# A two-layer attention trunk on one core: turned keys and queries kept as scaled fp16 pairs, key pairs copied by DMA

## The chip, the cores and the metric

The kernel runs on one core of a Trainium2 chip. The metric is the device time of one execution in microseconds; a quoted time is the median of several runs. Beside the timed runs stands one profiled execution, from which all rows in this document come.

## The reference, cut to what matters

Two layers over 512 latent tokens (8 x 64) and 256 context tokens, width 1024, all in fp32. Each layer normalises its input, modulates it, and multiplies it by one wide matrix `w_in`; the product holds keys, values and queries of two attentions (heads of 64), the silu paths and the merge gates.

```
hx = rmsnorm(x, g) * (1 + scale) + shift;  px = hx @ w_in          # hc, pc likewise for the context
qa, ka = rmsnorm(a_q, q_norm_a), rmsnorm(a_k, k_norm_a)            # 8 heads
s = [ qa . ka(window 8 x 16) / 8 + bias  |  qa . cka / 8 ]         # A: neighbourhood and context keys
a = softmax(s) @ values
qb, kb = rope(rmsnorm(b_q, q_norm_b)), rope(rmsnorm(b_k, k_norm_b))  # 8 query heads, 2 key heads
b = softmax(qb . [ckb, kb] / 8) @ values                           # B: all latent and context keys
out = (sigmoid(g_a) * ((a * silu(a_z)) @ w_o_a) + sigmoid(g_b) * ((b * silu(b_z)) @ w_o_b)) @ w_out
x = x + gate * out
```

In layer 0 the context tokens go through the same (they read context keys only); layer 1 updates the latent tokens alone.

## The kernel before, in words

All 768 tokens of a layer stay in SBUF, as six tiles of 128 tokens, already normalised and transposed, each number as a pair of fp32r tiles, high and low (`hx`). Weights come in tiles of 128 x 512 (`load_w`, L397, and `load_w2`, L412): SyncE's DMA queue (SP) loads `raw`, ScalarE casts it to `whi`, and VectorE or GpSimd subtracts for `wlo`. A projection takes three matmuls for each of eight weight tiles (`mm3`, L433): high by high, high by low, low by high.

The order within a layer, and what carries it in the code:

- **Projections of attention A** (from L705): the keys for the six token tiles, the values (`C_AV`, from L756), the queries (`C_AQ`, from L767). A tile's sums of squares go through ScalarE, VectorE and GpSimd (`head_rstd`, L510), then VectorE scales the heads, and the tile is put on a list of late work. `turn` (L524) is that late work: four TensorE transposes into a PSUM tile of the pool "t" (two buffers), and one ScalarE pass that writes fp32 channels by tokens into `ka` or `qa`, with the norm's weight as scale. `perm` shifts the latent queries by 64 tokens, so that tiles 0 and 3 are written in two pieces.
- **Attention A** (`pipeline`, L1013, with `na_first` L1034): head by head, the scores of head h and then the values of head h - 1, with chunks of other projections as fill between them. For each head `stage_k` (L865) makes fp32r pairs of the keys from `ka`, in one of two pairs of tiles, and `stage_q` (L874) a tile whose one half holds the high part of the head's queries and whose other half holds the low part; `kh` is written twice, once for each half of the 128 rows, so that one matmul by `kh` gives the high and the low query part, and one by `kl` adds the low key part (`scores`, L883, and L974). `load_bias` (L948) loads the head's relative position bias; VectorE adds it and takes the maximum (L977), ScalarE takes the exponential, and the probabilities are split into fp16 halves (`turned`, L831) and turned by transposing DMAs on SP's queue. In layer 0 each head has context scores as well (`ctx_scores`, L892).
- **Projections of attention B** (from L1064): keys and values (`evac_bkv`, L1085), then the queries (`evac_bq`, L1120), with the rotary turn in `rope_heads` (L578). `stage_k` runs once for each of the two key heads, after query tiles 1 and 2, and fills `gk`.
- **Attention B** (L1148 to L1201): the same pipeline, with `stage_q` for each head, scores over all 768 keys, and the maximum against the constant `lift` (L1157).
- **Merge and output** (from L1204).

Beside this, steps of the adaLN product run in the background: `ada_steps` (L278) loads a tile of `w_ada` (`rawb`, two buffers) on SP's queue and reduces it on VectorE, behind the VectorE instruction issued last (`behind`, L473). In layer 0 the steps for the output gate come in two halves, one beside the projections of B (L1099), one in attention B (L1200). Their loads have no such order, neither before nor after the change.

In `start` (L1287) each engine keeps the order of the program. Everywhere else a planner, which goes through the program with a simulated timeline, orders the instructions of every engine and of the DMA queues, and gives out the buffers: of 9 tiles of 128 x 3072 fp32 (`big`, L91) each tensor such as `ka`, `va`, `qa`, `za`, `vb` or `gk` takes one.

Of the kernel before, what the change touches and what calls it, by code (L numbers as in the profile page):

```python
# [34 lines left out]
P_UP = 2.0 ** 14  # L35
SPLIT_POOL = (1, 3)
# [20 lines left out]
def F(ap):  # L57
    return ap.bitcast(F32)
# [14 lines left out]
def hybrid_kernel(es: ExitStack, tc, x, ctx, cvec, w_ada, w_ada0, small, gvec, w_in, w_o_a, w_o_b, w_out,  # L73
# [56 lines left out]
    cd = drp.tile([16, 128], F32, name="cd")  # L130
    gs = [drp.tile([128, 4, NTOK], F32, name=f"gs{c}") for c in range(4)]
# [55 lines left out]
    G.memset(ehalf, -0.5)  # L187
# [39 lines left out]


# [295 lines left out]
    def turn(y, npair, dst, t, perm, g):  # L524

        n = 128 * npair
        pt = psw(n, "t")
        for j in range(npair):
            T.transpose(pt[:, 128 * j:128 * j + 128], y[:, 128 * j:128 * j + 128], ident)
        if perm and t in (0, 3):  # L530

            src = pt.rearrange("p (j s n) -> p j s n", j=npair, s=2)
            d = dst[:, :, 0:512].rearrange("p j (s n) -> p j s n", n=64)
            if t == 0:
                d = d[:, :, 0:3:2, :]
            else:
                src, d = src[:, :, ::-1, :], d[:, :, 1:8:6, :]
        else:
            c0 = 128 * t + (64 if perm and t < 4 else 0)
            src = pt.rearrange("p (j n) -> p j n", j=npair)  # L540
            d = dst[:, :, c0:c0 + 128]
        if g is None:
            S.copy(d, src)
        else:
            S.activation(d, src, AF.Copy, scale=g)
# [49 lines left out]
    def layer(l, hx, nxt, start):  # L595
# [110 lines left out]
        kav = big("ka").rearrange("p (j n) -> p j n", j=4)  # L706
        if first:
# [7 lines left out]
            def evac_ak(ts):  # L715
# [9 lines left out]
                for i, t in enumerate(ts):  # L725
                    mul_heads(ys[t], ys[t], ss[:, 8 * i:8 * i + 8], 8)
                    to_channels(ys[t], 4, kav, t, False, gk)
# [3 lines left out]
        else:  # L731
# [3 lines left out]
            for t in range(6):  # L735
                tok_proj(w, 512, a_hx, t, evac_na(kav, False, gk, 4))
# [19 lines left out]
        w = load_w(W, C_AV, 512, KT, mix_lo)  # L756
        for t in range(6):
            tok_proj(w, 512, a_hx, t, evac_va)
            if first:
# [6 lines left out]
        qav = big("qa").rearrange("p (j n) -> p j n", j=4)  # L766
        w = load_w(W, C_AQ, 512, KT, mix_lo, own=hp["p"])  # L767
        za = big("za")
# [6 lines left out]
        for t in range(qt):  # L775
            tok_proj(w, 512, a_hx, t, evac_na(qav, True, gq, YB if first else 4))
# [10 lines left out]
        if True:  # L787
# [68 lines left out]
            def k_tile(e, zero):  # L856
                kh = att["p"].tile([128, 768], F32R, tag=f"kh{e}", name=nm("kh"), bufs=1)
                kl = att["p"].tile([128, 768], F32R, tag=f"kl{e}", name=nm("kl"), bufs=1)
                if zero:
                    V.tensor_scalar(rows(kl, 1 - e).rearrange("p (a b) -> p a b", b=128),  # L860
                                    rows(ident, 1 - e).unsqueeze(1).to_broadcast([64, 6, 128]),
                                    0.0, None, ALU.mult)
                return kh, kl

            def stage_k(src, e, kh, kl, dup):  # L865

                k = rows(src, e)
                V.tensor_copy(rows(kh, e), k)
                S.copy(rows(kh, 1 - e), k)
                (G if dup else V).tensor_tensor(rows(kl, e), k, F(rows(kh, e)), ALU.subtract)  # L870
                if dup:
                    S.copy(rows(kl, 1 - e), F(rows(kl, e)))

            def stage_q(src, e):  # L874

                n = 768 if first else 512
                qs = att["p"].tile([128, n], F32R, tag=f"qs{e}", name=nm("qs"), bufs=1)
                q = rows(src, e)[:, :n]
                S.copy(rows(qs, e), q)
                V.tensor_tensor(rows(qs, 1 - e), q, F(rows(qs, e)), ALU.subtract)  # L880
                return qs
# [10 lines left out]
            def ctx_scores(q, kh, kl, ct, late=True):  # L892
# [7 lines left out]
                if late:  # L900
# [625 lines left out]
```

## Time and profile before

| | us |
|---|---|
| median of 3 runs | 1111.63 (1110.95 to 1113.45) |
| the profiled execution | 1110.55 |
| its span, first to last instruction | 1108.8 |
| TensorE busy in it | 1074.5 (97%) |
| VectorE busy | 767.4 (69%) |
| ScalarE busy | 617.2 (56%) |
| GpSimd busy | 470.1 (42%) |

Times in rows are us from the start of the span, and ns where a row gives the mean or the minimum, median and maximum of one instruction. PE is TensorE's matmul, PEld its weight load, DVE VectorE, ACT ScalarE, POOL GpSimd, SPq the queue of SyncE. L974 is line 974 of the kernel before. A row of a line or tile reads: line, engine, operation, out<-in by the program's names, count, duration. In brackets stands how long the engine had been idle and what ended that. Matmuls overlap, so the distance between two of them, not the duration of one, is what the stream costs.

### The profile page before, as it was taken

To read this page: it belongs to the slowest core of one execution; us is meant where nothing else is said; L and a number is where in the kernel's file an instruction comes from. 1 tells how busy PE (TensorE), PEld (TensorE's weight loads), DVE (VectorE), ACT (ScalarE), POOL (GpSimd) and SP (SyncE) were. 2 spreads that over 40 slices of the span, in tenths; PEclk is the share of its full clock that TensorE was granted. 3 is DMA by queue.
4 is the path that set the end of the run, shared out by engine and by line. 5 is a ranking of instruction groups with operands and counts; after the bars stand their busy time and mean duration, and the time that the engine had idled before them with its cause. 6 is when DMAs were issued, how large, how long until landed. Compare 5 with 4: busy or idle time off the path is not lost. (4 is left out here: it accounts for less than half of the span.)

```text
span 1108.8 us, 16943 instructions
## 1 busy us (share of the span) xinstructions
PE 1074.5 (97%) x5672; PEld 876.9 (79%) x5672; DVE 767.4 (69%) x1600; ACT 617.2 (56%) x1236; POOL 470.1 (42%) x397
## 2 busy tenths in 40 slices
PE   8999999899999999979999999999999999999998
PEld 6688888788888877757788878888877888777677
DVE  5567799974378478676577785466997665777473
ACT  6464279776333566655330275444899446786430
POOL 1044235554256244454521455232355472564531
PEclk9999999999999999989999999999999999999999
DMA  9454325554543498769533542453565536879642
GB/s 374 153 169 143 91 70 116 125 137 121 174 141 117 132 205 185 172 185 271 171 105 125 166 136 82 138 165 99 132 148 130 156 106 171 200 232 236 188 152 77
DMA packets 236001, 171.79 MB, mean 155 GB/s; under 512 B 160141, under 2 KB 201865, under 8 KB 234249
## 3 DMA queue, kind: packets, MB, share of 16 engines
q1 hardware_dynamic: 228576, 156.31, 51.7%
q0 software_dynamic: 2368, 7.87, 2.2%
q10 hardware_dynamic: 4968, 6.53, 1.8%
q8 instruction: 45, 0.74, 0.3%
q14 instruction: 44, 0.35, 0.1%
HBM read 115.58 MB, written 17.32 MB: 120 GB/s over the span
## 5 line engine op out<-in xcount | busy, mean ns | idle before, releaser
L838 POOL TENSOR_TENSOR h<-p,h 128x256 f16<-128x256 f32 (+2 forms) x104 | 113.1, 1096 | 167.7 <-ACT h L837 119.9
L422 POOL TENSOR_TENSOR wlo<-raw,whi 128x512 fp32r<-128x512 f32 x70 | 98.8, 1416 | 124.5 <-ACT whi L420 80.9
L435 PE MATMUL psf<-hx,whi 128*128 128x512 f32 (+1 forms) x360 | 137.5, 382 | 2.5 <-ACT zt L625 1.3
L437 PE MATMUL psf<-hx,wlo 128*128 128x512 f32 (+1 forms) x360 | 135.5, 376 | 0.0
L436 PE MATMUL psf<-hx,whi 128*128 128x512 f32 (+1 forms) x360 | 135.4, 376 | 0.0
L435 PE MATMUL psx<-whi,hx 128*128 128x512 f32 (+1 forms) x328 | 121.0, 372 | 0.0
L420 ACT CAST whi<-raw 128x512 fp32r<-128x512 f32 x136 | 82.9, 620 | 67.5 <-DMA raw<-in_w_in_dram 48.3
L437 PE MATMUL psx<-whi,hx 128*128 128x512 f32 (+1 forms) x328 | 120.0, 367 | 0.0
L436 PE MATMUL psx<-wlo,hx 128*128 128x512 f32 (+1 forms) x328 | 119.6, 366 | 0.0
L408 POOL TENSOR_TENSOR wlo<-raw,whi 128x512 fp32r<-128x512 f32 x40 | 59.5, 1489 | 119.2 <-ACT whi L405 76.0
L405 ACT CAST whi<-raw 128x512 fp32r<-128x512 f32 x88 | 54.2, 623 | 96.8 <-PE psx L437 34.2
L508 POOL TENSOR_TENSOR ss<-ss,ehalf 128x8 f32<-128x8 f32 (+2 forms) x40 | 63.6, 1593 | 77.8 <-DVE ss L505 72.5
L422 DVE TENSOR_TENSOR wlo<-raw,whi 128x512 fp32r<-128x512 f32 x66 | 70.8, 1073 | 35.2 <-ACT whi L420 34.1
L837 ACT CAST h<-p 128x256 f16<-128x256 f32 (+2 forms) x136 | 81.6, 616 | 7.7 <-DMA ct<-h 3.7
L435 PEld LDWEIGHTS psf<-hx,whi 128*128 128x128 f32 x360 | 67.8, 188 | 15.1 <-ACT zt L625 2.5
L1157 DVE CUSTOM_DVE_ANT_0 p<-pss,vb 128x768 f32<-128x768 f32 x64 | 60.4, 954 | 25.4 <-PE pss L887 22.7
L1158 ACT ACTIVATE p<-pss,mx 128x768 f32<-128x768 f32 x64 | 57.6, 901 | 35.7 <-DVE mx L1157 34.8
L437 PEld LDWEIGHTS psf<-hx,wlo 128*128 128x128 f32 x360 | 67.8, 188 | 11.8
L436 PEld LDWEIGHTS psf<-hx,whi 128*128 128x128 f32 x360 | 67.9, 189 | 10.7
L437 PEld LDWEIGHTS psx<-whi,hx 128*128 128x128 f32 x328 | 61.9, 189 | 10.2
L436 PEld LDWEIGHTS psx<-wlo,hx 128*128 128x128 f32 x328 | 62.0, 189 | 9.4
L435 PEld LDWEIGHTS psx<-whi,hx 128*128 128x128 f32 x328 | 61.8, 189 | 9.1 <-issue 0.2
(338 smaller groups left out, 2972.4 us busy)
## 6 DMA issues: line engine op xcount, KB each, us to landing
raw<-in_w_in_dram SPq DMA_DIRECT2D x168, 256.0 KB, 2.9
rawb<-in_w_ada_dram SPq DMA_DIRECT2D x48, 256.0 KB, 2.8
raw<-in_w_out_dram SPq DMA_DIRECT2D x32, 256.0 KB, 2.9
tg<-gs SPq DMA_DIRECT2D x4, 1536.0 KB, 7.1
rawx<-in_w_ada_dram SPq DMA_DIRECT2D x4, 1024.0 KB, 10.7
rawy<-in_w_ada_dram SPq DMA_DIRECT2D x4, 1024.0 KB, 9.3
gs<-zt ACTq DMA_DIRECT2D x16, 256.0 KB, 2.9
raw<-in_w_o_a_dram SPq DMA_DIRECT2D x16, 256.0 KB, 3.1
```

The lines of the kernel that those rows point to most:

```text
L405: S.copy(hi[:, :n], raw[:, :n])
L408: e.tensor_tensor(lo[:, :n], raw[:, :n], F(hi[:, :n]), ALU.subtract)
L420: S.copy(hi, raw)
L422: lo_eng(i).tensor_tensor(lo, raw, F(hi), ALU.subtract)
L435: T.matmul(ps, lhs[0], rhs[0], start=first, stop=False)
L436: T.matmul(ps, lhs[0], rhs[1], start=False, stop=False)
L437: T.matmul(ps, lhs[1], rhs[0], start=False, stop=last)
L508: G.tensor_tensor(ss, ss, ehalf[:, :n], ALU.pow)
L837: S.copy(h[:, 0], p[:, :n])
L838: eng.tensor_tensor(h[:, 1], p[:, :n], h[:, 0], ALU.subtract)
L1157: V.tensor_tensor_reduce(p, pss, lift, -1.0, 3e38, ALU.add, ALU.min, mx[:, 0:1])
L1158: S.activation(p, pss, AF.Exp, bias=mx[:, 0:1], accum_out=r[:, i:i + 1])
```

## The change

Keys and queries are no longer kept in fp32 and split head by head. `turn` writes a pair of fp16 tiles straight from PSUM: ScalarE the high part, VectorE the product less the high part. For keys the pair keeps all 128 channels of two heads. For queries each half of the channels (one head) is treated apart, so that one tile holds the high part of one head in its own 64 rows and the low part in the other 64; that is the layout which the scores multiply by, and `stage_q` is gone. `stage_k` is now two DMAs on SP's queue, each of which copies the head's 64 rows of both key parts into one half of the tile; the rows of the low key part that were zero now hold it a second time. For fp16 the numbers are scaled: the weights of the norms are scaled so that their largest entry becomes 2^11 (`head_scales`), the products are brought back where the maximum and the exponential are taken (`na_dq`, `gq_dq`), and the bias of A is scaled up once in each layer, through `za` and a copy in DRAM (`scale_bias`, issued after value tile 3, behind ScalarE's last instruction). `za` takes its buffer earlier, ahead of `qa`.

```diff
@@ turn
-        if g is None:
-            S.copy(d, src)
-        else:
-            S.activation(d, src, AF.Copy, scale=g)
+        def pair(hi, lo, x, g):
+            if g is None:
+                S.copy(hi, x)
+                V.tensor_tensor(lo, x, hi, ALU.subtract)
+            else:
+                S.activation(hi, x, AF.Copy, scale=g)
+                V.scalar_tensor_tensor(lo, x, g, hi, ALU.mult, ALU.subtract)
+        kind, a, b = dst
+        for n0, n1, c0 in cuts:
+            x = pt.rearrange("p (j n) -> p j n", j=npair)[:, :, n0:n1]
+            da, db = [d[:, :, c0:c0 + n1 - n0] for d in (a, b)]
+            if kind == "k":
+                pair(da, db, x, g)
+                continue
+            for e, d in enumerate((da, db)):
+                own, other = slice(64 * e, 64 * e + 64), slice(64 - 64 * e, 128 - 64 * e)
+                pair(d[own], d[other], x[own], None if g is None else g[own])
@@ layer, beside the values of A
+        nc.sync.dma_start(ti, bias_int[l].rearrange("h p n -> p h n"))
+        nc.sync.dma_start(te, bias_edge[l].rearrange("h p n -> p h n"))
+        def scale_bias():
+            for c in range(3):
+                c0 = 1024 * c
+                S.activation(za[:, c0:c0 + 1024], za[:, c0:c0 + 1024], AF.Copy, scale=na_up[:, l:l + 1])
+            nc.sync.dma_start(b_int[l].rearrange("h p n -> p h n"), ti)
+            nc.sync.dma_start(b_edge[l].rearrange("h p n -> p h n"), te)
...
+            if t == 3:
+                behind(ON_ACT, scale_bias)
@@ stage_k, stage_q
-                k = rows(src, e)
-                V.tensor_copy(rows(kh, e), k)
-                S.copy(rows(kh, 1 - e), k)
-                (G if dup else V).tensor_tensor(rows(kl, e), k, F(rows(kh, e)), ALU.subtract)
-                if dup:
-                    S.copy(rows(kl, 1 - e), F(rows(kl, e)))
+                for half in range(2):
+                    nc.sync.dma_start(rows(to, half), rows(src, e)[:, :, j, :])
-                S.copy(rows(qs, e), q)
-                V.tensor_tensor(rows(qs, 1 - e), q, F(rows(qs, e)), ALU.subtract)
+            def q_pair(src, e, j):
+                return src[:, e, j, :]
@@ attention A
-            akt = [k_tile(e, True) for e in range(2)]
+            akt = [att["p"].tile([128, 2, 768], F16, name=nm("kk"), bufs=1) for _ in range(2)]
-                    V.tensor_tensor_reduce(p[:, :512], pss, bedg if i == 0 else bint, -1.0, 3e38,
+                    V.tensor_tensor_reduce(p[:, :512], pss, bedg if i == 0 else bint, na_ndq[:, l:l + 1], 3e38,
@@ attention B
+            S.copy(g_abs, gbc)
+            head_scales(g_abs, g_inv, g_up)
...
-                    V.tensor_tensor_reduce(p, pss, lift, -1.0, 3e38, ALU.add, ALU.min, mx[:, 0:1])
-                    S.activation(p, pss, AF.Exp, bias=mx[:, 0:1], accum_out=r[:, i:i + 1])
+                    V.tensor_tensor_reduce(p, pss, lift, gq_ndq, 3e38, ALU.add, ALU.min, mx[:, 0:1])
+                    S.activation(p, pss, AF.Exp, bias=mx[:, 0:1], scale=gq_dq, accum_out=r[:, i:i + 1])
@@ new
+    def head_scales(rows, inv, up):
+        S.activation(rows, rows, AF.Abs)
+        V.tensor_reduce(inv, rows, AX, ALU.max)
+        V.tensor_scalar(inv, inv, G_MIN, 1.0 / H_UP, ALU.max, ALU.mult)
+        V.reciprocal(up, inv)
```

`na_scales`, which calls `head_scales` for the weights of A and makes the factors of both layers, is called in `start` behind the fourth weight tile; its rows come by one more load at the very start, on ScalarE's queue.

More of the change, by code (lines that the diff above doesn't have):

```diff
@@ L35 @@
 P_UP = 2.0 ** 14
+H_UP = 2.0 ** 11
+G_MIN = 1.0e-6
 SPLIT_POOL = (1, 3)
@@ L130, in hybrid_kernel @@
     cd = drp.tile([16, 128], F32, name="cd")
+    b_int = [drp.tile([8, 128, 256], F32, name=f"b_int{i}") for i in range(2)]
+    b_edge = [drp.tile([8, 128, 128], F32, name=f"b_edge{i}") for i in range(2)]
     gs = [drp.tile([128, 4, NTOK], F32, name=f"gs{c}") for c in range(4)]
```

109 lines of the change are left out of this document (56 added, 53 removed).

## The prediction

> **What bounds the kernel now.** I read the page's part 1 first, then the windows by stage, then single rows of the timeline.
>
> ```profile
> span 1108.8 us, 16943 instructions
> ...
> PE 1074.5 (97%) x5672; PEld 876.9 (79%) x5672; DVE 767.4 (69%) x1600; ACT 617.2 (56%) x1236; POOL 470.1 (42%) x397
> ```
>
> TensorE is the bound: of 1108.8 us of span it is idle for 34.3. No other engine is above 69% over the whole, but the share is a mean over unlike stages, so the windows come next (columns: span of the stretch, busy time and instruction count of PE, PEld, DVE, ACT, POOL, granted clock, DMA share, GB/s).
>
> ```profile
> 119.00:149.00 30.00, 30.00 (x161) 25.50 (x160) 24.15 (x57) 10.51 (x17) 6.42 (x5) 1.00 0.26 77
> 200.00:250.00 50.00, 46.94 (x286) 39.60 (x284) 41.64 (x108) 37.74 (x86) 26.18 (x31) 1.00 0.54 132
> 330.00:375.00 45.00, 45.00 (x233) 37.90 (x233) 28.47 (x49) 16.70 (x27) 23.68 (x14) 1.00 0.41 129
> 420.00:480.00 60.00, 56.22 (x325) 45.73 (x325) 42.76 (x79) 39.80 (x80) 27.32 (x20) 1.00 0.74 169
> 480.00:545.00 65.00, 55.08 (x280) 41.50 (x279) 44.20 (x63) 33.38 (x65) 35.87 (x26) 0.92 0.75 204
> 830.00:880.00 50.00, 47.60 (x311) 40.29 (x312) 37.44 (x103) 35.97 (x85) 25.48 (x30) 1.00 0.57 147
> 980.00:1040.00 60.00, 57.53 (x269) 42.53 (x268) 43.74 (x69) 41.93 (x75) 40.50 (x27) 1.00 0.95 246
> ```
>
> The projections of the query stage (119 to 149, 330 to 375) keep PE busy throughout. The two attentions do not: the neighbourhood attention of layer 0 loses 3.06 us in the second window and that of layer 1 loses 2.40, the grouped one 3.78, 9.92 and, in layer 1, 2.47. So 21.6 of the 34.3 idle us lie in attention, and half of that in one stretch, where also the granted clock is 0.92, the only one under 1.00. Its cause stands in three rows of the timeline (start, duration, engine):
>
> ```profile
> 483.66 8.22 DVE L422 TENSOR_TENSOR wlo<-raw,whi 128x512 fp32r<-128x512 f32 x1
> 491.91 0.95 DVE L880 TENSOR_TENSOR qs<-qb,qs 64x768 fp32r<-64x768 f32 x1
> 493.56 0.69 PE L849 MATMUL psv<-ident,r 128*128 128x128 f32 x2 [5.79 <-DVE ho L825]
> ```
>
> One split on VectorE lasted 8.22 us; behind it in order stood `qs` and then the `ho` that PE waited 5.79 us for. The lower clock (0.08 of 65 us, 5.2) lies around that gap.
>
> **The change part by part.** First, the score matmuls. Their operands become fp16 instead of fp32r. Row counts of the high half, the low half being as many:
>
> ```profile
> L886 PE MATMUL pss<-gk,qs x144: 276/283/775, 374.1 to 1022.9; 128*128 128x256 f32 x80, 128*128 128x512 f32 x64
> L886 PE MATMUL pss<-kh,qs x48: 218/282/418, 149.5 to 841.9; 128*128 128x128 f32 x16, 128*128 128x384 f32 x16, 128*128 128x256 f32 x16
> L974 PE MATMUL pss<-kh,qs x48: 387/392/486, 150.0 to 847.6; 128*128 128x512 f32 x48
> ```
>
> That is 2 x 240 = 480 matmuls. What one costs is its distance to the next, not its modelled duration. fp32r rows and fp16 rows stand close together in one head:
>
> ```profile
> 161.98 0.39 PE L974 MATMUL pss<-kh,qs 128*128 128x512 f32 x1
> ...
> 162.68 0.39 PE L974 MATMUL pss<-kl,qs 128*128 128x512 f32 x1
> ```
> ```profile
> 164.38 0.28 PE L887 MATMUL pss<-kl,qs 128*128 128x256 f32 x1
> ```
> ```profile
> 164.62 0.28 PE L887 MATMUL pss<-kl,qs 128*128 128x256 f32 x1
> ```
> ```profile
> 169.92 1.04 PE L998 MATMUL psv<-ht,va 128*128 128x512 f16 x4
> ```
> ```profile
> 291.19 0.61 PE L921 MATMUL psv<-ht,va 128*128 128x256 f16 x4
> ```
> ```profile
> L998 PE MATMUL psv<-ht,va x56: 376/379/390, 169.9 to 863.5; 128*128 128x512 f16 x56
> L921 PE MATMUL psv<-ht,va x32: 269/273/283, 176.8 to 291.5; 128*128 128x256 f16 x32
> ```
>
> fp32r at 512 columns: first to last of four, 0.70 / 3 = 0.233; at 256: 0.24 / 2 = 0.120. fp16: (1.04 - 0.38) / 3 = 0.220 and (0.61 - 0.273) / 3 = 0.112. The difference is 0.013 and 0.008; I take 0.011 for each, 480 x 0.011 = **5.3 us** (3.8 to 6.2), all on the path, as PE has no slack.
>
> Second, the splits per head go (L868, L869, L870 for keys, L879, L880 for queries), and a split at the turning comes. Rows of the first attention, and the nearest rows of what is added (VectorE reading PSUM and an SBUF tile; ScalarE at the turning; a pass over 1025 columns):
>
> ```profile
> L869 ACT CAST kh<-ka x16: 830/832/836, 142.8 to 832.3; 64x768 fp32r<-64x768 f32 x16
> L868 DVE CAST kh<-ka x16: 542/557/1083, 144.1 to 831.2; 64x768 fp32r<-64x768 f32 x16
> L870 DVE TENSOR_TENSOR kl<-ka,kh x16: 939/955/1587, 145.3 to 832.6; 64x768 fp32r<-64x768 f32 x16
> ```
> ```profile
> L879 ACT CAST qs<-qa x16: 617/726/836, 144.5 to 833.2; 64x768 fp32r<-64x768 f32 x8, 64x512 fp32r<-64x512 f32 x8
> L880 DVE TENSOR_TENSOR qs<-qa,qs x16: 685/954/1673, 146.3 to 835.1; 64x768 fp32r<-64x768 f32 x8, 64x512 fp32r<-64x512 f32 x8
> L545 ACT ACTIVATE qa<-pst,gcol x10: 674/682/688, 114.9 to 764.5; 128x512 f32<-128x512 f32 x10
> ```
> ```profile
> L627 DVE SCALAR_TENSOR_TENSOR za<-za,psf x6: 673/682/686, 140.7 to 773.2; 128x512 f32<-128x512 f32 x6
> L627 DVE SCALAR_TENSOR_TENSOR za<-za,psx x6: 400/418/689, 142.0 to 767.5; 128x256 f32<-128x256 f32 x4, 128x512 f32<-128x512 f32 x2
> ```
> ```profile
> L357 ACT ACTIVATE junk<-x x6: 1057/1061/1068, 4.8 to 19.4; 128x1025 f32<-128x1025 f32 x6
> ```
>
> Removed on VectorE: 16 x 0.557 + 16 x 0.955 + (8 x 0.954 + 8 x 0.685) = 37.3, and 13.1 more for the second attention's sixteen query splits at the same price (an estimate): 50 us. On ScalarE: 16 x 0.832 + 2 x (8 x 0.836 + 8 x 0.617) = 36.6. All of it sat inside the attention loops, 2.5 us of VectorE per head ahead of that head's scores. Added on VectorE in the projections: 12 key tiles x 0.682; 10 + 10 query tiles in two halves each, four of them in quarters of 256 columns, 16 x 2 x 0.682 + 4 x 4 x 0.418; 12 small key tiles at 0.3 as an estimate: 8.2 + 28.5 + 3.6 = 40. ScalarE gets one pass more for each query tile, 20 x 0.68, and three bias passes a layer, 6 x 1.06: 20 us. What hides this is the PE work of the projections. The thinnest cover is 119 to 149: VectorE 24.15 of 30; five tiles add 5 x 1.36 = 6.8 and the first two heads' splits leave with 2 x 2.47 = 4.9, so 26. That fits. If it does not, PE waits for a turning buffer, up to about 3 us in a layer; I take +1 in all. The norms' scales are some ten narrow operations, put in the first 60 us and ahead of the rotary tables; hidden, at most 2 us.
>
> Third, what goes from the 21.6 idle us. The stall above is worth 10 (9.92 of idle time, with the slow clock inside it). The `qs` in it goes surely (0.95); the 8.22 is not touched by the change, but what stood in front shifts. Ends 0 and 10; I take 4, nearer to the row that stays than to nothing left. Of the other 11.7 I take a third, **4**, as VectorE loses 2.3 us a head in the first attention and 0.8 in the second, ScalarE 1.5 and 0.7.
>
> In sentences of its own: the Trainium skill, "GPSIMD Engine Reference", section Specifications, says that GpSimd's SBUF interfaces are shared with VectorE and that they contend where a VectorE instruction has two SBUF inputs. By it the removed `kl` and `qs` (maximum 1587 and 1673 ns beside 955) were exposed and the new splits, with one input in PSUM (maximum 686 in the row of L627), would not be; the third term would then be nearer 8 than 4.
>
> Fourth, DMAs. Each head of the first attention gets two copies of 64 partitions x 3 KB, each key group of the second two; each layer two bias loads and two stores of 1.5 MB in all. Nearest rows (issue times on SP's queue; landing; a wait):
>
> ```profile
> L842 SPq DMA_TRANSPOSE ht<-h x144: 1170/1284/7011, 155.8 to 1034.1; - x144
> ```
> ```profile
> L949 SPq DMA_DIRECT2D bint<-in_bias_int_dram x16: 340/526/1672, 135.0 to 844.0; - x16
> ```
> ```profile
> bedg<-in_bias_edge_dram SPq DMA_DIRECT2D x32, 32.0 KB, 2.2
> ```
> ```profile
> zb<-zs SPq DMA_DIRECT2D x1, 1536.0 KB, 6.7
> ```
> ```profile
> SPq L290 <- DVE asum L297: 90.9, 31, 9.5
> ```
> ```profile
> L943 DVE MEMSET bint<- x2: 272/272/272, 141.3 to 760.6; 128x256 f32 x2
> ```
>
> A copy costs SP about 0.53, so 1.1 us per head beside five or six transposes of 1.28. A head's two copies hold 384 KB; between the rows of 32 and 1536 KB that is 2.2 + 4.5 x 352 / 1504 = 3.3 us to landing. The two key tiles alternate, so a copy may go as soon as the scores two heads back are done, a head's length ahead: 16.4 us in layer 0 (L921 above, four rows a head, (291.5 - 176.8) / 7), and in layer 1 about 10.9, from the memset at 760.6 to the last L974 at 847.6 in eight. The bias (6.7 in, about as much out, 3.2 of ScalarE) has the rest of the value and query projections. Below zero is excluded, since nothing is removed from this queue; above, each copy could be late. I take **+2** for some late landings and later transposes.
>
> The Trainium skill, "SBUF - State Buffer", section Door 1, states that 64 partitions reach only half of the DMA ports. No run here shows a large transfer of 64 partitions; by that rule the part that grows with size doubles, 4.4 us to landing in place of 3.3, which the cover above still takes.
>
> Sum: -5.3 - 4 - 4 + 1 + 2 = -10.3. The profiled execution took 1110.55 for its span of 1108.8, so 1100.2; the median of the runs shown, 1111.63, is 1.1 above it: **1101**.
>
> **The rivals.**
> *Less VectorE work frees attention wholly:* the stall and its slow clock go (10), and half of the other idle time (6): -5.3 - 16 + 1 = -20, 1091. For it: half of the idle time has one cause. Against: the 8.22 us split is untouched.
> *The saved work was not on the path:* PE's own idle rows name `ho`, not `qs`. Only the matmuls gain, and the copies cost 2 to 4: 1107 to 1111.
> *SP's queue takes over; slower.* In before, SP already stood 90.9 us for one kind of load, the gate's weights, up to 9.5 at once, with everything behind it. If a head's copies are queued behind such a load or behind the previous head's last transposes, scores wait for an issue and a landing, 0.53 + 3.3, less what PE still has to do (I take two thirds of it): 1.3 us a head for 16 heads, 21 us, and gaps as long as that at 493 bring the slow clock again. -5.3 + 21 + 1 = +17, or +6 where only half the heads are hit: 1116 to 1128. It decides when the copies are issued later than about 4 us before PE is done with the previous head.
> *The change doesn't speed the scores:* the distance of matmuls is set by something else than the type. Then only the waits: -5, 1107.
>
> **How the numbers follow.** Forecast 0.39 (1096 to 1106), freed wholly 0.14, not on the path 0.13, SP's queue 0.29, no faster scores 0.05. About 0.2%, 2.2 us, is what a measurement of this kernel can tell from no change, 1109.4 to 1113.9. Faster: 0.39 + 0.14 + 0.05 + 0.05 = 0.63; same 0.08, the rest of "not on the path"; slower 0.29. The range leaves out the far third of the slow case and the far end of the fast one: 1089 to 1122.
>
> **What would show it.** Score matmuls of 512 columns 0.220 apart and of 256 0.112; PE busy throughout in the projections; windows of attention with less idle time and no clock under 1.00; waits of PE for a key copy near zero. It is wrong if PE or its loads wait for the key copies, if SP waits longer than 9.5 us in front of them, if VectorE fills the query projections above 0.95, or if a new stall like that at 484 stands elsewhere.

## The result, and the profile after

The changed kernel takes **1139.96 us** (median of 4 runs, 1138.47 to 1141.07), the kernel before 1112.3 us on the same chip: a ratio of 1.0248, 95% interval 1.0230 to 1.0267. It is slower by about 27 us, where 1101 was forecast and 1122 was the end of the range. The profiled execution took 1141.07 us.

The page of the changed kernel, first and third line:

```profile
span 1139.3 us, 16953 instructions
...
PE 1078.3 (95%) x5672; PEld 847.5 (74%) x5672; DVE 758.2 (67%) x1627; ACT 608.5 (53%) x1219; POOL 450.1 (40%) x393
```

VectorE's busy time fell by 9 us and ScalarE's by 9, as the change intends in kind. PE is idle for 61.0 us instead of 34.3, and busy for 3.8 us more although its score matmuls became shorter. The windows show where. First the kernel before, by stage: start and projections of A in layer 0, attention A and attention B of layer 0, projections of A in layer 1, attention A and attention B of layer 1 (from the first score to the last value matmul); columns as in the prediction.

```profile
0.00:149.50 149.50, 146.27 (x756) 114.11 (x757) 100.35 (x238) 75.60 (x143) 42.08 (x38) 1.00 0.51 173
149.50:291.50 142.00, 138.89 (x847) 118.02 (x846) 107.41 (x293) 105.73 (x240) 69.07 (x74) 1.00 0.53 132
...
374.10:537.90 163.80, 149.72 (x828) 119.16 (x827) 113.72 (x203) 103.23 (x200) 75.07 (x53) 0.97 0.79 192
...
651.50:774.60 123.10, 123.10 (x578) 101.53 (x578) 74.21 (x129) 61.32 (x117) 44.27 (x32) 1.00 0.40 121
774.60:864.40 89.80, 87.02 (x460) 68.88 (x460) 76.73 (x215) 78.28 (x173) 42.73 (x47) 1.00 0.57 140
...
923.50:1044.00 120.50, 117.10 (x554) 88.09 (x553) 80.06 (x128) 83.66 (x149) 66.71 (x44) 1.00 0.85 210
```

The same stages of the changed kernel:

```profile
0.00:156.10 156.10, 149.37 (x761) 116.41 (x761) 109.83 (x260) 80.90 (x154) 40.54 (x38) 0.98 0.59 192
156.10:296.10 140.00, 136.99 (x839) 111.12 (x838) 94.24 (x281) 97.57 (x228) 65.61 (x74) 0.99 0.63 149
...
379.90:538.80 158.90, 142.43 (x816) 105.80 (x816) 108.95 (x196) 102.50 (x194) 73.04 (x53) 0.98 0.82 196
...
655.80:782.10 126.30, 124.37 (x578) 100.90 (x576) 79.72 (x143) 69.06 (x132) 43.01 (x33) 1.00 0.50 153
782.10:890.80 108.70, 93.31 (x486) 67.04 (x485) 64.97 (x195) 72.16 (x161) 40.99 (x47) 0.97 0.56 138
...
948.50:1072.10 123.60, 116.60 (x546) 78.89 (x546) 79.46 (x123) 82.18 (x142) 64.07 (x43) 0.97 0.86 210
```

Attention A of layer 1 grew from 89.8 to 108.7 us, **18.9 of the 30.5 us** that the span grew. PE's idle time there rose from 2.8 to 15.4 us, and its clock fell from 1.00 to 0.97, while VectorE, ScalarE and GpSimd have less to do there than before. The start is 6.6 us longer, the projections and attention B of layer 1 each 3 us, and output and merge of layer 0, where nothing was edited, 3.4 (113.6 to 117.0); both attentions of layer 0 are shorter, by 2.0 and 4.9. Differences of 3 us in one stage say little: in the thirteen profiles of the changed kernel and its variants in which PE runs attention B of layer 1 in the same order, that stage lasts between 120.1 and 123.8 us.

Two things came as the prediction had them. The scores are faster; four of 512 columns in a row (the timeline of the changed kernel):

```profile
802.78 1.03 PE L1002 MATMUL pss<-kk,qa 128*128 128x512 f16 x4
```

With 0.38 for the last, (1.03 - 0.38) / 3 = 0.217 apart, against 0.233 before. And PE hardly waits for the key copies. Its matmuls waited 0.4 us for them, all in this group, and its weight loads 1.8 us in two places:

```profile
L914 PE MATMUL pss<-kk,qa 128*128 128x128 f16 x16 | 3.6, 225 | 1.2 <-DVE r L838 0.8 <-DMA kk<-ka 0.4
```

The largest single loss in attention A of layer 1 is elsewhere. SP's queue and PE in the timeline of the changed kernel:

```profile
846.15 14.13 SPq L889 DMA_TRANSPOSE ht<-h  x10
860.33 0.57 SPq L662 DMA_DIRECT2D gs<-zt  x1
861.00 0.94 SPq L442 DMA_DIRECT2D raw<-in_w_in_dram  x2
```
```profile
864.78 0.80 PE L460 MATMUL psx<-hx,whi 128*128 128x512 f32 x1 [6.12 <-ACT whi L445]
```

PE stood 6.12 us for the weights of the fill. They were issued at 861, behind ten transposes and a store; they landed, ScalarE cast them, and only then PE went on. The delay is in the queue: the tiles that the weights go into were free from 847.5 on, when the last split that read one ended, and from 847.4 to 861 SP issued with hardly a gap.

### The profile page after: what moved, and what is told of

Read it like the earlier page. It is cut to its first block, busy times and chain, and to the rows that moved or that the text cites. A ratio compares the mean times of both kernels' runs of the same rounds, so it can differ in the third digit from the quotient of the medians.

```text
span 1139.3 us, 16953 instructions
## 1 busy us (share of the span) xinstructions
PE 1078.3 (95%) x5672; PEld 847.5 (74%) x5672; DVE 758.2 (67%) x1627; ACT 608.5 (53%) x1219; POOL 450.1 (40%) x393
## 5 line engine op out<-in xcount | busy, mean ns | idle before, releaser
L885 POOL TENSOR_TENSOR h<-p,h 128x256 f16<-128x256 f32 (+2 forms) x104 | 108.5, 1052 | 165.9 <-ACT h L884 123.9
L447 POOL TENSOR_TENSOR wlo<-raw,whi 128x512 fp32r<-128x512 f32 x70 | 95.9, 1373 | 131.3 <-ACT whi L445 96.9
L460 PE MATMUL psf<-hx,whi 128*128 128x512 f32 (+1 forms) x360 | 139.4, 387 | 4.0 <-DVE za L660 2.2
L461 PE MATMUL psf<-hx,whi 128*128 128x512 f32 (+1 forms) x360 | 136.8, 380 | 0.0
L447 DVE TENSOR_TENSOR wlo<-raw,whi 128x512 fp32r<-128x512 f32 x66 | 75.2, 1140 | 54.1 <-ACT whi L445 53.0
L433 POOL TENSOR_TENSOR wlo<-raw,whi 128x512 fp32r<-128x512 f32 x40 | 59.0, 1479 | 127.0 <-ACT whi L430 74.3
L1195 ACT ACTIVATE p<-pss,mx,vb 128x768 f32<-128x768 f32 x64 | 63.5, 992 | 44.7 <-DVE mx L1194 44.1
L1194 DVE CUSTOM_DVE_ANT_0 p<-pss,vb 128x768 f32<-128x768 f32 x64 | 64.2, 1013 | 19.4 <-PE pss L915 17.1
L460 PE MATMUL psx<-hx,whi 128*128 128x256 f32 (+1 forms) x208 | 70.7, 340 | 6.2 <-ACT whi L445 6.1
L462 PE MATMUL psx<-hx,wlo 128*128 128x256 f32 (+1 forms) x208 | 70.0, 336 | 1.3 <-DVE wlo L447 1.1
## 6 DMA issues: line engine op xcount, KB each, us to landing
rawy<-in_w_ada_dram SPq DMA_DIRECT2D x4, 1024.0 KB, 10.9
```

Source lines behind the costliest of these rows:

```text
L433: e.tensor_tensor(lo[:, :n], raw[:, :n], F(hi[:, :n]), ALU.subtract)
L447: lo_eng(i).tensor_tensor(lo, raw, F(hi), ALU.subtract)
L460: T.matmul(ps, lhs[0], rhs[0], start=first, stop=False)
L461: T.matmul(ps, lhs[0], rhs[1], start=False, stop=False)
L462: T.matmul(ps, lhs[1], rhs[0], start=False, stop=last)
L885: eng.tensor_tensor(h[:, 1], p[:, :n], h[:, 0], ALU.subtract)
```

## The experiments

In the expectations "idle time of PE" in a stage is the distance of its matmuls from one to the next beyond their distance at full clock, summed; it holds what the half clock costs too, and gives 5.3 us for attention A of layer 1 before and 22.0 after, where the windows, span less busy time, give 2.8 and 15.4. Below I use the length of that stage, from windows with the columns above, and the ratio to the kernel before on the same chip. In every run the planner orders all engines again, so a run differs from its neighbour by more than its edit; where that bears on a reading, the text gives how many matmuls keep their order.

The first theory: SP's queue, in order and already well filled in attention A of layer 1, cannot take the key copies, and what stands behind them comes late (theory 1); beside it, the load of the gains at the start delays what follows (theory 2). Its rivals: the transfers themselves load the DMA engines, whoever issues them (rival 1), or the copies are bystanders and the planner moved other work (rival 2).

**First four runs.**

Copies on ACT's queue:

```diff
-                stage_k(kav, j, e, akt[e])
+                stage_k(kav, j, e, akt[e], (nc.sync if first else S))
```

> The changed kernel with one edit: in attention A of layer 1 the two key copies of each head (L906) are issued by ACT's queue instead of SP's. Theory 1 (SP's queue is the bound of that stage; the 16 copies, about 0.77 us of issue each in the changed kernel's trace, 9 to 12 us in all, push the fill's weight loads and the transposes late): the idle time of PE in attention A of layer 1 falls from 22 us to about 6 to 10, the 6.3 us wait of the score tiles' fill for whi L445 is gone, and the kernel takes 1122 to 1130 us. Rival 1 (the copies cost by their landing or by the DMA engines they occupy, whoever issues them): 1136 to 1142 us. Rival 2 (the planner put other work late, and the copies are a bystander): 1136 to 1142 us with the stage still over 105 us.

```profile
781.70:883.70 102.00, 92.69 (x484) 65.26 (x484) 65.01 (x196) 70.70 (x162) 42.20 (x47) 0.98 0.62 151
```

1130.49 us, 1.0177 (1.0162 to 1.0192); the 6 us wait for weights is gone. About 8 us come back, less than half of the loss; the theory expected 10 to 18.

Stores on ACT's queue:

```diff
-                    (nc.sync if not first else G if silu else S).dma_start(spill[:, f, n0:n1], d)
+                    (S if not first else G if silu else S).dma_start(spill[:, f, n0:n1], d)
```

> The changed kernel with one edit: the stores of the gate and z chunks in layer 1 (L662) are issued by ACT's queue instead of SP's, and the key copies stay on SP's. Theory 1 (SP's issue time in attention A of layer 1): about ten stores of some 0.6 us leave the queue, so 5 to 6 us of the stage's 16.7 us loss come back, 1132 to 1136 us. Rivals 1 and 2: no change, 1138 to 1142 us.

1136.57 us, 1.0225 (1.0205 to 1.0244), the stage 104.9 instead of 108.7. That is 2.6 us less where theory 1 expected 5 to 6, and the interval overlaps that of the changed kernel (1.0230 to 1.0267): a hint that a relief without touching the copies helps, and no more.

Dummy copies in the kernel before:

```diff
-                stage_k(kav[:, j, :], e, kh, kl, False)
+                stage_k(kav[:, j, :], e, kh, kl, False); _ = [nc.sync.dma_start(rows(spare, half), rows(kav[:, j, :], e)) for half in range(2) if not first]
```

> The kernel before with one addition: in attention A of layer 1, SP's queue issues two copies more for each head, of the same size and shape of partitions as the changed kernel's key copies (64 partitions, 192 KB), into a tile that nothing reads. Theory 1 (SP's queue): the stage loses 8 to 17 us and the kernel takes 1119 to 1130 us, with waits for weights and transposes in that stage. Rival 2 (other work moved, not the queue): 1111 to 1114 us. Rival 1 (what they occupy on the DMA engines) would slow it as well, so this run speaks only against rival 2.

```profile
777.00:873.30 96.30, 90.06 (x460) 68.31 (x460) 78.38 (x215) 79.08 (x174) 43.77 (x47) 1.00 0.66 155
```

1119.23 us, 1.0078 (1.0062 to 1.0093): slower by 8.6 us, 6.5 of them in this stage, though no engine reads a dummy and only eight of them were issued within the stage. The queue itself waited for them: it stood 4.9 us in this stage until the dummy before, which writes the same tile, had landed. Rival 2 as it was expected, with no loss at all, falls. That the planner's new order has a part in the loss (396 of 459 matmuls of the stage keep theirs) is not excluded.

The gains' load later:

```diff
-    S.dma_start(nrow.rearrange("p g d -> p (g d)"), gvec[:, 256:512].to_broadcast([128, 256]))
...
-                                ada_load(7)
+                                ada_load(7); nc.sync.dma_start(nrow.rearrange("p g d -> p (g d)"), gvec[:, 256:512].to_broadcast([128, 256]))
```

> The changed kernel with one edit: the load of the row of norm gains (nrow, L194) is taken off ACT's queue at the start and issued by SP's queue at the third step of the opening projection (L1470), where its first reader is still ahead. Theory 2 (the one DMA more at the start makes the second load of x wait for that of the identity and everything after it lands 1.4 us later, and the TensorE clock halves for another 6.8 us): the start's idle falls from 22 us to about 16 and the kernel takes 1132 to 1136 us. Rival: the start's loss comes from something else, such as the scales computed there: 1138 to 1142 us.

1138.89 us, 1.0245 (1.0210 to 1.0280). **Theory 2 falls.** The start still takes 155.6 us, though SP issues the third load of x at 3.05 us again and not at 5.32.

**Four more.** Two of them ask why the move to ACT's queue gave back so little.

Keys written by engines, in layer 1:

```diff
-                    nc.sync.dma_start(rows(to, half), rows(src, e)[:, :, j, :])
+                    (nc.sync.dma_start if dma else (S.copy, V.tensor_copy)[half])(rows(to, half), rows(src, e)[:, :, j, :])
...
-                stage_k(kav, j, e, akt[e])
+                stage_k(kav, j, e, akt[e], first)
```

> The changed kernel with one edit: in attention A of layer 1 the two key copies of a head are no DMAs any more; ScalarE writes the one half and VectorE the other. Theory 1, as the first four runs leave it (the copies cost by SP's issue time, some 6.6 us in the stage, and by what they add to the DMA engines, which lengthened every other issue there): the idle time of PE in the stage falls from 22 us to 5 to 9, less than the 15.4 that it had with the copies on ACT's queue, and the kernel takes 1119 to 1127 us. If the copies cost by SP's issue time alone, the run equals the one with the copies on ACT's queue or is slower by the engines' work: 1129 to 1134 us. Rival 2 (other work moved): above 1134 us.

```profile
784.40:874.50 90.10, 87.19 (x474) 63.89 (x474) 68.36 (x201) 77.71 (x166) 41.61 (x47) 0.98 0.56 141
```

1123.28 us, 1.0107 (1.0088 to 1.0126): 16 us come back, and the stage is as long as before the change, 90.1 against 89.8. So making the copies by DMA accounts for the whole loss of this stage. What is open is by which way: by the queue, by the DMA engines, or by the order that the planner makes with them.

Copies and stores on ACT's queue, and the gains' load later (the three edits above together):

> The changed kernel with three edits together: copies of attention A in layer 1 and stores of the gate and z chunks in layer 1 on ACT's queue, and the load of the norm gains at the third step of the opening projection. Theory 1 with SP's issue time as the main cost: both reliefs add, 10 to 13 us against the changed kernel, 1125 to 1129 us, with 11 us of idle time left in the stage. If what the copies add to the DMA engines is the rest, the stores' move does nothing more: 1129 to 1132 us.

1131.20 us, 1.0182 (1.0157 to 1.0208), the stage 102.7: no more than the copies' move alone.

Split on VectorE:

```diff
-            hilo(za, gated["a"], range(4))
+            hilo(za, gated["a"], range(4), V if first else G)
```

> The changed kernel with one edit: the low parts of the gated values of branch a in layer 0 (L701, four subtractions of 768 columns) are made by VectorE instead of POOL. The traces of both kernels show one VectorE split of 0.69 us lasting 8.22 and 8.35 us beside an unbroken row of POOL's work, and PE idle for 6 us behind it. If POOL's row is what holds VectorE, the wait of 6 us at 492 goes, and the time falls by 3 to 7 us, to 1133 to 1137 us. Rival: the VectorE work added, four times about 1 us, takes its place: 1138 to 1142 us.

The changed kernel's stall, VectorE and POOL in the timeline, with PE's wait:

```profile
489.30 8.35 DVE L447 TENSOR_TENSOR wlo<-raw,whi 128x512 fp32r<-128x512 f32 x1 [0.46 <-ACT whi L445]
```
```profile
487.63 7.13 POOL L701 TENSOR_TENSOR gal<-za,gah 128x768 fp32r<-128x768 f32 x4
494.73 1.25 POOL L447 TENSOR_TENSOR wlo<-raw,whi 128x512 fp32r<-128x512 f32 x1
495.95 1.14 POOL L885 TENSOR_TENSOR h<-p,h 128x512 f16<-128x512 f32 x1
```
```profile
498.15 0.69 PE L896 MATMUL psv<-ident,r 128*128 128x128 f32 x2 [5.81 <-DVE ho L872]
```

POOL in the kernel before, beside the split of 8.22 us at 483.66:

```profile
482.98 7.12 POOL L668 TENSOR_TENSOR gal<-za,gah 128x768 fp32r<-128x768 f32 x4
490.05 1.27 POOL L422 TENSOR_TENSOR wlo<-raw,whi 128x512 fp32r<-128x512 f32 x1
```

The same split in the changed kernel when VectorE makes `gal` itself:

```profile
492.45 0.68 DVE L447 TENSOR_TENSOR wlo<-raw,whi 128x512 fp32r<-128x512 f32 x1
```

1128.21 us, 1.0153 (1.0134 to 1.0172): 11 us less than the changed kernel, where 3 to 7 were expected. The split lasted 0.68 us again, though nothing in it was edited: POOL's unbroken row had held it. In both kernels the split ended 0.56 us after that row did (491.88 and 491.32, 497.65 and 497.09). Over all eighteen profiles, none of the 1150 splits of this size that VectorE began beside an idle POOL lasted more than 0.85 us, and all 636 longer ones began beside POOL's work (410 more began so and were not stretched). This agrees with the rule of the Trainium skill that the prediction cites ("GPSIMD Engine Reference", section Specifications), with 8.35 against 0.68 us beside it. Attention B of layer 0 has 12.3 idle us instead of 16.5, but with more matmuls in it is only 0.9 us shorter (158.0). Most of the gain came in stages that the edit doesn't touch (output and merge of layer 0 from 117.0 to 111.0 us, the projections after them from 126.3 to 122.9), where the planner's order changed; so the run shows what held the split, and not that this is worth 11 us.

The bias as it is given:

```diff
-                nc.sync.dma_start(bint[:, 0:256], b_int[l][h])
+                nc.sync.dma_start(bint[:, 0:256], bias_int[l, h])
...
-            if t == 3:
-                behind(ON_ACT, scale_bias)
```

> The changed kernel without the scaling of the bias tables: it reads both tables as they are given, leaves out the two loads, three ScalarE passes and two stores of each layer, so the bias is added without the heads' factor. Theory: these lie beside projections that PE fills and cost nothing or up to 2 us, 1137 to 1141 us; the 3 us that PE lost at the start of layer 1's projections stay. Rival: the 3 MB that the two layers send through the queue push the weights late, and 4 to 6 us come back: 1133 to 1136 us.

1128.89 us, 1.0162 (1.0134 to 1.0191). Both expectations miss, the theory by 8 us and its rival by 4. The start is 3.0 us shorter, and its wait for `za`, 2.2 us at 145 in the changed kernel, is 0.8. The rest can't be put down to the scaling: attention A of layer 1 is 6.0 us shorter with 341 of its 485 matmuls in the old order, and attention B of layer 1 is 2.8 us shorter with the same order in every engine. PE's waits at the start of layer 1's projections stay, as expected.

**Four on the remainder.** With copies on ACT's queue VectorE waited for the bias tables in attention A of layer 1:

```profile
DVE p L1005 <- DMA bint<-b_int: 8.5, 4, 3.4
...
DVE p L1005 <- DMA bedg<-b_edge: 4.0, 2, 3.7
```

Two bias tiles:

```diff
+            btab = [[att["p"].tile([128, 512], F32, name=nm(b), bufs=1) for b in ("bint", "bedg")] for _ in range(2)]
...
+                bint, bedg = btab[h % 2]
```

> The changed kernel with one edit: the two bias tables of attention A are kept in two tiles each, by the head's parity, so that a head's tables can be loaded while the head before still reads its own. The runs with the copies or the stores on ACT's queue left 15 to 18 us of idle time of PE in attention A of layer 1, and there VectorE waited 12.5 to 14.9 us for bias tables (1.3 in the kernel before, 4.5 with the copies made by the engines). Theory 3: the new scores start a head sooner than SP's queue, behind the copies, brings the single tiles; then this run gets back 5 to 12 us, 1127 to 1134 us. If the late tables only follow from the copies' load on queue and DMA engines, it brings 0 to 3 us, 1136 to 1140 us.

1130.38 us, 1.0181 (1.0160 to 1.0202), the stage 100.3: theory 3 seems to hold. The next run speaks against it.

> The changed kernel with the bias tables in two tiles each and the key copies of attention A in layer 1 on ACT's queue. Theory 3: the idle time of PE in the stage falls from 15.4 us (copies on ACT's queue alone) to 6 to 9, as with copies made by the engines, 1120 to 1125 us. If what the copies add to the DMA engines is the rest: 1128 to 1132 us, as with the copies on ACT's queue alone.

```profile
785.00:883.80 98.80, 89.79 (x471) 64.20 (x470) 66.53 (x195) 70.75 (x161) 40.96 (x47) 0.97 0.64 150
```

1128.65 us, 1.0165 (1.0128 to 1.0202). VectorE's wait for tables fell from 12.5 to 2.8 us, and the stage is still 9 us longer than with engine copies. **Theory 3 falls** as the main cause: late tables are one of several things that come late.

The parts together: engine copies in attention A of both layers, the split on VectorE, the later load:

> The changed kernel with three edits: the key copies of attention A made by ScalarE and VectorE in both layers, the low parts of branch a's gated values in layer 0 by VectorE, and the load of the norm gains at the third step of the opening projection. If the gains of the parts add (16.7 us for the engines' copies in layer 1, 11.7 for the split on VectorE, 1 for the load): 1109 to 1114 us, the time of the kernel before or a little above. If part of the split's gain was the order that the whole program took with it, 1114 to 1120 us.

```profile
154.20:289.20 135.00, 135.00 (x840) 109.26 (x839) 96.79 (x289) 106.83 (x237) 66.11 (x74) 1.00 0.57 140
...
768.80:856.70 87.90, 85.56 (x473) 62.90 (x473) 66.64 (x200) 77.14 (x166) 41.12 (x47) 1.00 0.58 145
```

1107.23 us, 0.9957 (0.9940 to 0.9973): **faster than both kernels**, 0.4% below the kernel before and 2 us better than the sum of the parts. In layer 0's attention A PE is never idle, 135.0 us instead of 142.0 before; in layer 1's it takes 87.9 instead of 89.8.

The same split in the kernel before:

> The kernel before with one edit, the low parts of branch a's gated values in layer 0 made by VectorE instead of POOL. If POOL's unbroken row is what holds VectorE's split there, the wait of 6 us at 487 with its slow clock goes in this kernel too: 1101 to 1106 us, faster than both kernels. If VectorE, busier in this kernel than in the changed one, pays it back: 1109 to 1113 us.

```profile
375.20:532.30 157.10, 142.70 (x816) 114.24 (x815) 113.71 (x206) 103.90 (x200) 69.15 (x49) 1.00 0.85 198
...
648.30:775.50 127.20, 125.02 (x579) 101.14 (x578) 76.27 (x133) 63.98 (x125) 43.64 (x33) 1.00 0.39 117
```

1111.84 us, 1.0014 (1.0000 to 1.0029): not faster. Attention B of layer 0 shrinks by 6.7 us, and the clock there is 1.00; but output and merge grow from 113.6 to 116.0 and the projections from 123.1 to 127.2. In these two stages the planner put the work in another order, which fits as what took the gain back; that order was not tried alone.

**Queue or transfer.** This pair keeps the engine copies and adds dummies, so that no score reads what a DMA brings:

```diff
-                stage_k(kav, j, e, akt[e])
+                stage_k(kav, j, e, akt[e], first); _ = [S.dma_start(rows(spare, half), rows(akt[e], half)) for half in range(2) if not first]
```

> The changed kernel with the key copies of layer 1's attention A made by the engines (1123.3 us, 5.9 us of idle time of PE in the stage), and two dummy copies for each head on ACT's queue: the same 64 partitions and 192 KB, from the finished key tile into a tile that nothing reads. If the transfers cost by what they occupy of the DMA engines, the stage loses 5 to 10 us again, 1128 to 1134 us. If the copies cost only by SP's order of issue or by the scores' wait for them: 1122 to 1126 us.

```profile
785.40:874.50 89.10, 83.62 (x451) 59.66 (x451) 67.75 (x200) 77.14 (x165) 41.67 (x47) 1.00 0.68 157
```

With `nc.sync` in place of `S`:

> The same with the dummy copies on SP's queue. If SP's order of issue is the cost, alone or beside the DMA engines: 1131 to 1141 us, above the run with the dummies on ACT's queue by 4 us or more. If only the DMA engines count, the two runs agree within 2 us. If the real cost is that the scores wait for keys that come by DMA, neither shows it: both 1122 to 1126 us.

```profile
786.30:895.90 109.60, 93.39 (x474) 65.99 (x474) 70.12 (x201) 78.42 (x166) 40.59 (x47) 0.91 0.57 141
```

On ACT's queue 1125.07 us, 1.0123 (1.0108 to 1.0138); on SP's 1145.25 us, 1.0294 (1.0276 to 1.0312). Against engine copies alone (1.0107) the same bytes between the same tiles cost 2 us at most on the one queue, though the DMA engines are busier there (0.68 instead of 0.56), and 21 on the other, more than any theory had put down, with a clock of 0.91 in the stage. **What they occupy on the DMA engines is not the cost (rival 1 falls).** What is left is their place in SP's queue, together with the order that the planner makes around it. The pair does not part these two: the two programs have only 325 of 449 and 472 matmuls of the stage in the same order. With the dummies on SP's queue, PE's longest wait in the stage came 29 us after the last dummy was issued:

```profile
883.62 3.26 DVE L447 TENSOR_TENSOR wlo<-raw,whi 128x512 fp32r<-128x512 f32 x1 [0.52 <-ACT whi L445]
...
892.93 1.44 PE L1026 MATMUL psv<-ht,va 128*128 128x512 f16 x3 [5.14 <-issue]
```

PE's next matmuls read transposes (`ht`) that SP issued from 887.61 to 891.43; for the wait itself the profile names no releaser. From 884.8 to 886.9 the queue had stood before a weight load, for whose tile this split had to end, and the split lasted 3.26 us beside a row of POOL's work. An entry that cannot start holds all behind it, and that entry need not be the one that was added.

Two variants of the version of 1107.2 us, the second with `stage_k(kbv, 0, e, gkt[:, e], False)`:

> The version with engine copies in attention A of both layers, the split on VectorE and the later load of the gains (1107.2 us), with the bias tables in two tiles each besides. VectorE waited 4.3 us for tables in its layer 1 stage, PE 0.9 us: 0 to 3 us less, 1104 to 1108 us. If a table loaded a head earlier only moves transposes back in SP's queue: 1107 to 1111 us.

> The same version (1107.2 us) with the four key copies of each layer's attention B made by ScalarE and VectorE as well, instead of by SP's queue. They are issued in the query projections, whose PE rows show no wait for them: no change that can be told apart, 1105 to 1109 us. If they delay the transposes behind them: 1102 to 1105 us.

1108.93 us, 0.9967 (0.9952 to 0.9983), and 1107.30 us, 0.9963 (0.9950 to 0.9976): neither can be told from 0.9957. With the queue relieved, earlier tables and engine copies in attention B bring nothing more.

## Why the prediction was wrong

**The step that failed is the fourth term, "+2" for the DMAs, and the question under it.** In place of 2 us the copies cost about 16 (1.0248 with them, 1.0107 with copies made by the engines in layer 1). The term priced a copy by its issue and its landing and asked whether the scores of the same head would wait for it. They hardly do: 0.4 us of the matmuls and 1.8 of the weight loads. Nor does the landing explain the loss. One copy of 192 KB landed in 3.8 us, last column of this row of the changed kernel's page; where a head's two were issued one right behind the other, the second had landed 3.9 to 5.1 us after the first was issued, which is longer than the 3.3 us of the working for the two and near the 4.4 that the Trainium skill's rule gave there ("SBUF — State Buffer", section Door 1):

```profile
kk<-ka SPq DMA_DIRECT2D x32, 192.0 KB, 3.8
```

It never asked how full SP's queue was in the stage with the shortest heads. The issue rows of the kernel before in attention A of layer 1 (minimum, median, maximum in ns):

```profile
L842 SPq DMA_TRANSPOSE ht<-h x40: 1170/1221/2080, 781.4 to 860.4; - x40
```
```profile
L417 SPq DMA_DIRECT2D raw<-in_w_in_dram x14: 367/438/579, 775.3 to 849.4; - x14
```
```profile
L951 SPq DMA_DIRECT2D bedg<-in_bias_edge_dram x14: 471/522/602, 776.1 to 839.8; - x14
```
```profile
L949 SPq DMA_DIRECT2D bint<-in_bias_int_dram x7: 341/534/1672, 786.6 to 844.0; - x7
```
```profile
L629 SPq DMA_DIRECT2D gs<-zt x6: 373/470/578, 823.9 to 863.3; - x6
```

40 x 1.221 + 14 x 0.438 + 14 x 0.522 + 7 x 0.534 + 6 x 0.470 = 68.8 us of 89.8 without the few others: the queue issued for over three quarters of the stage, in order, and any wait of an entry holds all behind it. Twelve copies came in between, each longer than a weight load and than the 0.53 us of the working:

```profile
L906 SPq DMA_DIRECT2D kk<-ka x12: 626/647/2093, 788.4 to 864.6; - x12
```

That is 7.8 us at the median, which by issue time alone the queue still had room for. The stage lost more than twice as much. In the rows, what came late behind other entries left PE idle, the weights above all (6.1 us), and after the long gap its clock was halved; how much of the rest is the queue and how much the planner's new order is not shown. The row of transposes with its x144 and the estimate "1.1 us per head beside five or six transposes of 1.28" stood in the prediction; the division by the length of a head, 10.9 us in layer 1, did not: 6.4 to 7.7 of transposes and 1.1 of copies, before any load or store.

**The rival "SP's queue takes over"** (0.29) had the right place and the wrong victim. It let the scores wait behind the gate's loads, with 16 heads alike and 21 us at most. In fact other DMAs were late behind the copies, in layer 1, where the gate's loads no longer run. So its 1128 was too low too. (Its lower end, 1116, should by its own +6 have been 1118.)

Point by point for the rest:

- *Scores, -5.3:* right. 0.217 apart for 512 columns, and the price per row is the one forecast.
- *The stall at 484, -4:* did not come. Split and wait are still there, 8.35 and 5.81 us, because their cause is POOL's row of `gal`, which the change doesn't touch. The prediction named the 8.22 as untouched and then took 4 all the same. The run with `gal` on VectorE shows what held the split.
- *Other idle time of attention, -4:* the work did leave VectorE, and with the copies out of the queue the gain is there in layer 0: PE is never idle in attention A, where it had lost 3.1 us, and the stage is 7.0 us shorter. In the change as made it was overlaid.
- *Projections, +1:* too low. Projections of A in layer 1 lost 3.2 us, the start 6.6. The cover that "fits" at 26 of 30 us was the thinnest indeed: in the same stretch of the changed kernel VectorE is busy for 27.80 of 30 us, and PE stood 2.2 us until VectorE had written `za`. Leaving the bias scaling out gave 10 us back over all stages (1.0248 to 1.0162), of which only the 3.0 of the start came where the scaling lies.

```profile
123.50:153.50 30.00, 27.80 (x144) 23.27 (x143) 27.80 (x65) 10.61 (x20) 6.35 (x4) 1.00 0.41 108
```

- *"No clock under 1.00":* wrong, and so the loss grew. It is not a separate cause; it follows gaps.
- *The signs of being wrong:* the one that came clearly is the new stall, 6.12 us at 864.78. The others ask about the copies themselves, and what the copies delayed was something else.

What stays open, beside the part of the planner's order: why copies on ACT's queue leave 12 us in the stage (102.0 against 90.1), when dummies there leave none. The orders of SP's queue differ. With copies on ACT's queue:

```profile
810.78 7.56 SPq L889 DMA_TRANSPOSE ht<-h  x5
818.43 0.54 SPq L977 DMA_DIRECT2D bint<-b_int  x1
```

With engine copies:

```profile
811.66 0.54 SPq L977 DMA_DIRECT2D bint<-b_int  x1
```

The planner, which sees a DMA in one program and two engine passes in the other, put five transposes ahead of a bias table in the first. That fits, but a program with the one order and the other copies wasn't run, so it is argued and not shown. What is left of the start's 6.6 was not traced to a cause either, and the 3 us of attention B in layer 1 lie within what that stage varies by. Of the loads of the gate halves without a tie nothing bad was seen: attention B of layer 0 became shorter; a version with the tie wasn't tried.

## What to carry to other kernels

Before a copy is moved from engines to DMA, add up the issue times of the queue that will carry it, over the shortest stage, and ask what stands behind the new entries rather than who reads them. To tell a full queue from busy DMA engines, send dummies that nobody waits for through two queues. Where a planner orders the whole program, a single edit moves stages that it never touches by 2 to 6 us either way, and reorders the stage that it does touch. So read a gain from the stage that was edited, ask whether the order there stayed, and trust the total only in the program that will be kept.

## What the runs showed of the hardware

PE's clock halves after a gap and stays so for some microseconds. The 6.12 us wait that ended at 864.78, in windows of the changed kernel:

```profile
862.70:869.50 6.80, 4.72 (x11) 3.79 (x12) 1.15 (x1) 2.39 (x4) 2.55 (x2) 0.50 0.95 274
```

The clock is 0.50 from 862.7 to 869.5, so more than 4 us of matmuls ran at half speed after the wait was over; a gap costs more than its length. A wait of 1.83 us was enough in attention B of layer 1 of the changed kernel, where PE had been busy for 2.27 of the 4.1 us before the drop:

```profile
1022.76 0.50 PE L460 MATMUL psf<-gah,whi 128*128 128x512 f32 x1 [1.83 <-DVE tg L736]
```
```profile
1019.00:1023.10 4.10, 2.27 (x15) 1.45 (x14) 4.04 (x6) 1.72 (x3) 3.64 (x3) 1.00 1.03 354
1023.10:1026.50 3.40, 3.40 (x10) 2.62 (x9) 2.66 (x5) 2.97 (x7) 0.24 (x2) 0.50 1.38 315
```

The Trainium skill, "TensorE: Matmul & The Clock Gate", section Part 1, puts the clock at half after an idle window of about 3.4 us, with windows that run freely. The stretches of 3.4 and 6.8 us agree with such windows; that a window must be idle throughout does not agree with the second case. Nor does a longer gap always do it: with the dummies on ACT's queue PE waited 2.7 us once in attention A of layer 1, and the clock there stayed 1.00. What parts the cases is how busy PE was in the window. The clock changes on a grid of 3.41 us; over all eighteen profiles, from 20 us on and up to the last stage, each of the 68 windows at full clock that a half clock followed had PE busy for at most 1.75 us, and no window with PE busy for less than 1.49 us was followed by full clock. Where no gap stood, as in layer 0's attention A of the version of 1107.2 us, the clock was 1.00.
